# Probability rows scaled on GpSimd, score operands split once for two heads and placed by DMA, and forgetting attention's head factors made for two pairs at a time

## The chip, the cores and the metric

One Trainium2 chip; the kernel runs on one of its cores. The time is that of the whole program on the device, in microseconds (us). TensorE (PE), VectorE (DVE), ScalarE (ACT), GpSimd (POOL) and SyncE (SP) each run their own instructions in a fixed order; in this kernel SP issues nearly all transfers.

## The reference

Two transformer blocks over 512 positions of width 1024, in float32. The first has a feed-forward network, a mixing layer (three-branch sparse attention with 16 query heads of width 64, a gated convolution, attention to a memory of 256 rows) and a second feed-forward network. The second block has two layers: stick-breaking attention and forgetting attention, each followed by a feed-forward network and a gate. The parts that the change touches:

```python
def rms_norm(x, g):
    y = x * lax.rsqrt(jnp.mean(x * x, axis=-1, keepdims=True) + EPS)
    return y * g
# sparse attention, selected blocks and window, a head at a time
s = einsum('qd,kd->qk', q, k) * scale + bias;  p = masked_softmax(s);  o = p @ v
out = gate_c * o_c + gate_s * o_s + gate_w * o_w
# stick-breaking attention
z = q @ k.T * scale;  w = exp(log_sigmoid(z) + later(z));  o = w @ v
# forgetting attention: q and k normalized for each head
logits = q @ k.T * scale + fb[:, None] - f_cum[None, :];  o = softmax(causal(logits)) @ v
```

## The kernel before

Activations are stored transposed, 128 features by 512 positions to a tile. Float32 products are made from pairs: `split` writes a rounded part `h` (ACT) and the rest `lo` (DVE, `src - h`), and a dense product is three matmuls (`mm3`, L221 to L223). Weights come in chunks of 128x1024: a DMA into `raw` (L209), in forgetting attention a multiplication by the gain on POOL (L213), then the split into `wh` and `wl` (L191, L201), each of the three tiles with three buffers. One 128x512 result takes 24 matmuls.

For the scores of two heads that share a 128-row tile, `stacked` (rounded part and rest of one head above each other) and `doubled` (the rounded part twice, and the rest with zeros) make operands of all 128 rows; they split each half of 64 rows by itself, and in `doubled` POOL writes the zeros (L357) and copies the rounded half to the other half (L359). `scores` then takes two matmuls for a tile of 128 queries (L371, L372).

In sparse and forgetting attention a head goes this way: scores into PSUM bank `s`, a DVE pass that adds the bias and finds the extreme (L525), an exponential on ACT that sums the row (L527), the reciprocal of the sums (L922, L1147), the scaling of the four probability tiles (L925, L1149: 128x128, 128x256, 128x384, 128x512), ten transpositions on PE into bank `t` (L774), their splits into `pth` and `ptl`, and eight products with the values (L781, L782). The products of one head are kept back in `self.rest` and are written into the program after the next head's scores.

`head_stats` squares the tiles, sums them for each head on PE (L316) and calls `rstd`, which makes the inverse root with an exponential and one Newton step; `head_norm` spreads the factors over the rows on PE (L334, L335) and multiplies on DVE (L336). In forgetting attention `lead(t)` makes key and query tiles of pair `t` (and every second time values for two pairs) and their factors, `norm` normalizes them and makes the operands, and `forget_head` runs twice. `lead(t + 1)` is written between `norm` of pair `t` and its heads.

The program is written in this order, but a scheduler at build time sets the order on each engine by its own account of when things are ready, so dense products of later pairs stand between the steps of a head.

Of the kernel before, what the change touches and what calls it, by code (L numbers as in the profile page):

```python
# [17 lines left out]
S = 512  # L18
# [144 lines left out]
class Net:  # L163
# [90 lines left out]
    def rstd(self, out, ss, n, rows=P):  # L254

        nc = self.nc
        v = self.t(self.sb, S, "nrv")[:rows, :n]
# [80 lines left out]

    def stacked(self, pool, x, tag, scale=None, bufs=None):

        out = []
# [7 lines left out]
    def doubled(self, pool, x, tag, scale=None, bufs=None):  # L349

        nc = self.nc
        out = []
        for b in range(2):
            z = self.t(pool, S, f"{tag}d{b}", bufs, F32R)
            lo = self.t(pool, S, f"{tag}l{b}", bufs, F32R)
# [95 lines left out]
    def setup(self):  # L451
# [6 lines left out]
        nc.vector.memset(self.ones_d, 1.0 / D)  # L458
        self.h = [self.pair(sb, f"h{c}") for c in range(KC)]
# [227 lines left out]
    def compress_flat(self, pool, tn, xs):  # L687
# [4 lines left out]
        for k in range(4):  # L692
# [10 lines left out]
            fh, flo = self.pair(pool, "pt", S, 2)  # L703
# [82 lines left out]
    def nsa(self):  # L786
        nc, tc = self.nc, self.tc
        with self.pool("nsa", "right") as pool:
# [41 lines left out]
            for j in range(4):  # L830
                self.head_norm(ks[j], j, 1, st, self.col("kg"))
            for a in range(2):
                kn = [self.doubled(pool, ks[2 * br + a], f"k{br}") for br in range(2)]
# [63 lines left out]
    def nsa_heads(self, pool, a, r, qn, kn, V, pc, G):  # L897
        nc = self.nc
        for b in range(2):
# [12 lines left out]
            for br in range(2):  # L912
# [11 lines left out]
                for i in range(NT):  # L924
                    nc.vector.tensor_scalar(pr[i], pr[i], st[:, i : i + 1], None, op0=ALU.mult)  # L925
# [61 lines left out]
    def stick(self):  # L987
        nc, tc = self.nc, self.tc
        self.log_exp_tables()
        with self.pool("sbk", "left") as pool:  # L990
            self.tags = self.TAGS
            m, V, rT = [], {}, self.t(pool, NT, "rT")

            def lead(t):
# [11 lines left out]
                return self.doubled(pool, qk[0], "q", 0.125, 2), self.stacked(pool, qk[1], "k", None, 2)  # L1006
# [68 lines left out]
    def forget(self):  # L1075
# [3 lines left out]
        with self.pool("fox", "left") as pool:  # L1079
# [17 lines left out]
            def lead(t):  # L1097
                if t % 2 == 0:
                    V[t // 2] = self.values(pool, self.a["w_fv"][t // 2], rT, gs)
                xs = []  # L1100
                for w, g in (("w_fk", gs), ("w_fq", ga)):
# [102 lines left out]
```

## Time and profile before

| | |
|---|---|
| median of 3 runs | 2964.11 us (2963.78 to 2964.3) |
| the profiled execution, its own time | 2958.98 us |
| its span, first to last instruction | 2957.2 us |
| PE busy | 2890.5 us |
| DVE busy | 1741.1 us |
| ACT busy | 1247.7 us |
| POOL busy | 191.3 us |

The profiled execution lies 5.1 us (0.17%) under the median, and 1.8 us of it lie outside the span. The parts of the span that the change touches: sparse attention from about 560 to 1050 us, stick-breaking attention from about 1490 to 1760 us, forgetting attention from about 2220 to 2530 us. The rest is dense work. The end of a matmul in the trace is modelled, so that matmuls overlap in it; how fast they follow each other is read from their starts.

### The profile page before, as it was taken

The page shows a single profiled execution, that of the slowest core. Times are in us where ns is not written, and L with a number is a line of the kernel's source. Part 1 is how long each engine was busy: PE and PEld are TensorE (multiplying, and loading weights), DVE is VectorE, ACT ScalarE, POOL GpSimd, SP SyncE. Part 2 cuts the span into 40 slices and gives each one's busy share as a digit, 9 for nine tenths or more (in the row PEclk, how much of TensorE's full clock was granted, in tenths as well). Part 3 has the DMA queues.
Part 4 walks back from the last instruction along what each step waited for, and adds up shares of the span by engine and source line. Part 5 has one row for each costly group of instructions (what it writes and reads, how often), then busy time and mean ns, then how long its engine had stood idle before and what let it go on. Part 6 is the DMA issues. An engine that isn't in the chain of part 4 may idle for free.

```text
span 2957.2 us, 36647 instructions
## 1 busy us (share of the span) xinstructions
PE 2890.5 (98%) x13874; PEld 2360.8 (80%) x13874; DVE 1741.1 (59%) x2997; ACT 1247.7 (42%) x2130; POOL 191.3 (6%) x245
## 2 busy tenths in 40 slices
PE   8999999999999999999999999999998998999999
PEld 8888887787877888888888877888887776788887
DVE  7434345778868755343358886443458997543334
ACT  6322234345646544222246664232244665432223
POOL 0000000001011010000012100000004311000000
PEclk9999999999999999999999999999999999999999
DMA  7432342232232345323331135323332223523322
GB/s 228 119 100 93 102 133 90 91 123 75 82 98 65 90 157 171 100 94 96 110 108 44 51 107 178 98 95 95 92 122 92 72 64 115 181 97 100 93 87 98
DMA packets 115946, 310.84 MB, mean 105 GB/s; under 512 B 13959, under 2 KB 26759, under 8 KB 115768
## 3 DMA queue, kind: packets, MB, share of 16 engines
q1 hardware_dynamic: 115096, 307.17, 32.8%
q10 hardware_dynamic: 672, 1.32, 0.4%
q8 instruction: 109, 1.79, 0.2%
q14 instruction: 69, 0.57, 0.1%
HBM read 279.82 MB, written 28.61 MB: 104 GB/s over the span
## 4 chain that ended last, share of the span: by engine, by line
PE 88%; DVE 7%; ACT 2%; DMA 1%; issue 1%; POOL 0%; SPq 0%; DVEq 0%; POOLq 0%; ACTq 0%
PE d L223 10%; PE d L222 10%; PE d L221 10%; PE o L221 5%; PE o L223 5%; PE o L222 5%; PE s L221 5%; PE s L222 5%; PE t L223 5%; PE t L221 5%; PE t L222 5%; PE s L223 5%; PE t L774 2%; DVE wl L201 1%; PE s L371 1%
## 5 line engine op out<-in xcount | busy, mean ns | idle before, releaser
L191 ACT ACTIVATE wh<-raw 128x1024 fp32r<-128x1024 f32 (+3 forms) x499 | 493.7, 990 | 1248.4 <-PE d L222 343.8
L201 DVE TENSOR_TENSOR wl<-raw,wh 128x1024 fp32r<-128x1024 f32 (+3 forms) x499 | 573.5, 1150 | 308.8 <-ACT wh L191 306.0
L191 ACT ACTIVATE pth<-t 128x512 fp32r<-128x512 f32 x144 | 70.5, 524 | 58.3 <-PE t L774 57.7
L774 PE MATMUL t<-idn,pr 128*128 128x128 f32 x480 | 85.7, 286 | 8.4 <-DVE ptl L201 3.7
L201 DVE TENSOR_TENSOR ptl<-t,pth 128x512 fp32r<-128x512 f32 x144 | 81.9, 596 | 13.1 <-ACT pth L191 11.9
L213 POOL TENSOR_TENSOR raw<-raw,cols 128x1024 f32<-128x1024 f32 x25 | 52.8, 2116 | 543.6 <-DMA xd<-x 483.2
L774 PEld LDWEIGHTS t<-idn,pr 128*128 128x128 f32 x480 | 56.9, 142 | 30.6 <-DVE ptl L201 11.4
L781 PE MATMUL o<-ptl,V 128*128 128x512 f32 x192 | 63.0, 339 | 0.0
L525 DVE CUSTOM_DVE_ANT_0 pr<-s,tb 128x128 f32<-128x128 f32 (+3 forms) x128 | 59.8, 482 | 4.1 <-PE s L372 3.1
L782 PE MATMUL o<-pth,V 128*128 128x512 f32 x192 | 57.5, 326 | 0.0
L415 DVE TENSOR_TENSOR ta<-t,ta 128x512 f32<-128x512 f32 x22 | 15.2, 692 | 70.9 <-PE t L223 70.8
L415 DVE TENSOR_TENSOR ta<-s,ta 128x512 f32<-128x512 f32 x22 | 15.2, 691 | 70.2 <-PE s L223 70.2
L221 PE MATMUL d<-h0h,wh 128*128 128x512 f32 x138 | 55.9, 405 | 0.5 <-ACT qs L191 0.4
L414 ACT ACTIVATE ta<-ta 128x512 f32<-128x512 f32 x88 | 55.3, 629 | 2.3 <-DVE ta L413 2.1
L415 DVE TENSOR_TENSOR ta<-o,ta 128x512 f32<-128x512 f32 x22 | 15.2, 692 | 68.4 <-PE o L223 67.4
L415 DVE TENSOR_TENSOR ta<-d,ta 128x512 f32<-128x512 f32 x22 | 15.2, 691 | 68.1 <-PE d L223 67.4
L223 PE MATMUL d<-h0h,wl 128*128 128x512 f32 x138 | 54.4, 394 | 0.8 <-DVE wl L201 0.8
L222 PE MATMUL d<-h4l,wh 128*128 128x512 f32 x138 | 54.7, 397 | 0.0
L222 PE MATMUL d<-h0l,wh 128*128 128x512 f32 x138 | 54.7, 396 | 0.0
L223 PE MATMUL d<-h4h,wl 128*128 128x512 f32 x138 | 54.6, 396 | 0.0
L222 PE MATMUL d<-h7l,wh 128*128 128x512 f32 x138 | 54.4, 394 | 0.0
L222 PE MATMUL d<-h3l,wh 128*128 128x512 f32 x138 | 54.4, 394 | 0.0
(2175 smaller groups left out, 8921.3 us busy)
## 6 DMA issues: line engine op xcount, KB each, us to landing
raw<-in_f_in_dram SPq DMA_DIRECT2D x176, 512.0 KB
raw<-in_f_out_dram SPq DMA_DIRECT2D x64, 512.0 KB
raw<-in_f_out_dram SPq DMA_DIRECT2D x32, 384.0 KB
raw<-in_w_mg_dram SPq DMA_DIRECT2D x24, 512.0 KB
raw<-in_w_cv_dram SPq DMA_DIRECT2D x24, 512.0 KB
xd<-x SPq DMA_DIRECT2D x40, 256.0 KB
x<-xd SPq DMA_DIRECT2D x40, 256.0 KB
raw<-in_w_pg_dram SPq DMA_DIRECT2D x16, 512.0 KB
```

The lines of the kernel that those rows point to most:

```text
L191: nc.scalar.activation(h, src, AF.Copy, scale=1.0 if scale is None else scale)
L201: eng.tensor_tensor(lo, src, hb, op=ALU.subtract)
L213: nc.gpsimd.tensor_tensor(v, v, gain.unsqueeze(2).to_broadcast([P, gain.shape[1], n]), op=ALU.mult)
L221: mm(out, lh, rh, start=first, stop=False)
L222: mm(out, lh, rl, start=False, stop=False)
L223: mm(out, ll, rh, start=False, stop=last)
L414: nc.scalar.activation(ta, ta, AF.Silu)
L415: nc.vector.tensor_tensor(ta, pb, ta, op=ALU.mult)
L525: nc.vector.tensor_tensor_reduce(out=p, in0=src, in1=bias, op0=ALU.add, op1=ALU.min, scale=1.0, scalar=3e38, accum_out=m)
L774: nc.tensor.transpose(tp[:, d : d + P], pr[i][:, j * P : (j + 1) * P], self.ident)
L781: nc.tensor.matmul(po[:, j * P :], v(j), pl[:, c], start=first and j == 0, stop=False)
L782: nc.tensor.matmul(po[:, j * P :], v(j), ph[:, c], start=False, stop=last and j == NT - 1)
```

## The change

It does these things. (1) `rstd` adds EPS inside the logarithm's bias and inside the last multiplication, with one DVE instruction less. (2) `stacked` and `doubled` split all 128 rows at once into `hv` tiles, and DMAs of 64x512 (four for `stacked`, six for `doubled`) place the halves; the zeroed rows of the `lo` tiles are written once. These DMAs stand in SP's queue with the weight loads. (3) The four probability tiles of a head are scaled by POOL instead of DVE. (4) In forgetting attention `lead(u)` makes two pairs of keys and queries, with one `head_stats` for four tiles, and is called after every second `norm` only. (5) `pth`/`ptl` have one buffer instead of two.

```diff
     def rstd(self, out, ss, n, rows=P):
-        nc.vector.tensor_scalar(v, ss, EPS, None, op0=ALU.add)
-        nc.scalar.activation(r, v, AF.Ln)
+        nc.scalar.activation(r, ss, AF.Ln, bias=self.eps[:rows])
...
-        nc.vector.tensor_tensor(t, t, v, op=ALU.mult)
+        nc.vector.scalar_tensor_tensor(t, ss, EPS, t, op0=ALU.add, op1=ALU.mult)
...
+    def halves(self, pool, x, scale):
+        h, lo = self.pair(pool, "hv", bufs=2)
+        self.split(h, lo, x, scale)
+        return h, lo
     def stacked(self, pool, x, tag, scale=None, bufs=None):
...
-            self.split(z[own], z[other], x[own], scale)
+            nc.sync.dma_start(z[own].bitcast(F32), h[own].bitcast(F32))
+            nc.sync.dma_start(z[other].bitcast(F32), lo[own].bitcast(F32))
...
-            nc.gpsimd.memset(lo[other].bitcast(F32), 0.0)
-            self.split(z[own], lo[own], x[own], scale)
-            nc.gpsimd.tensor_scalar(z[other], z[own].bitcast(F32), 1.0, 1.0, op0=ALU.mult, op1=ALU.mult)
-            out.append((z, lo))
+            nc.sync.dma_start(z[own].bitcast(F32), h[own].bitcast(F32))
+            nc.sync.dma_start(z[other].bitcast(F32), h[own].bitcast(F32))
+            nc.sync.dma_start(los[b][own].bitcast(F32), lo[own].bitcast(F32))
+            out.append((z, los[b]))
...
-        ph, pl = self.pair(pool, "pt", 1280, 2)
+        ph, pl = self.pair(pool, "pt", 1280, 1)
...
-                    nc.vector.tensor_scalar(pr[i], pr[i], st[:, i : i + 1], None, op0=ALU.mult)
+                    nc.gpsimd.tensor_scalar(pr[i], pr[i], st[:, i : i + 1], 1.0, op0=ALU.mult, op1=ALU.mult)
...
+            def lead(u):
+                V[u] = self.values(pool, self.a["w_fv"][u], rT, gs)
                 xs = []
-                for w, g in (("w_fk", gs), ("w_fq", ga)):
...
+                for t in (2 * u, 2 * u + 1):
+                    for w, g in (("w_fk", gs), ("w_fq", ga)):
...
                 return xs, self.head_stats(xs, self.sel64, 1, pool=pool)
...
-                k, q = norm(*ahead)
-                if t + 1 < KC:
-                    ahead = lead(t + 1)
+                k, q = norm(t, *ahead)
+                if t % 2 and t + 1 < KC:
+                    ahead = lead(t // 2 + 1)
```

The order of PE near the end of forgetting attention, where the factors of pair 6 have been spread and its scores follow. `h`, `m` with a number are activations of a dense product, `kd`, `kl`, `qs` the score operands. Before, these rows stand ahead of the scores:

```order
L223 MATMUL d_21196<-h5h_81,wl_21201 128x512
L221 MATMUL d_21196<-h6h_83,wh_21200 128x512
L222 MATMUL d_21196<-h6l_84,wh_21200 128x512
L223 MATMUL d_21196<-h6h_83,wl_21201 128x512
L221 MATMUL d_21196<-h7h_85,wh_21200 128x512
L222 MATMUL d_21196<-h7l_86,wh_21200 128x512
L223 MATMUL d_21196<-h7h_85,wl_21201 128x512
L316 MATMUL s_21230<-nrq_21232,sr_156 16x512
L316 MATMUL s_21230<-nrv_21233,sr_156 16x512
L371 MATMUL s_21267<-kd_4118_21144,qs_4122_21156 128x256
```

They are the last of 48 dense matmuls of pair 7 that stand between the spreading (L334, L335) of pair 6 and its scores. Now the same place reads, from the last product of pair 5 on:

```order
L801 MATMUL o_21039<-pth_21040,V_19938 128x128
L221 MATMUL d_21651<-m4h_20574,wh_21654 128x512
L222 MATMUL d_21651<-m4l_20575,wh_21654 128x512
L223 MATMUL d_21651<-m4h_20574,wl_21655 128x512
L221 MATMUL d_21651<-m0h_21245,wh_21654 128x512
L222 MATMUL d_21651<-m0l_21246,wh_21654 128x512
L223 MATMUL d_21651<-m0h_21245,wl_21655 128x512
L388 MATMUL s_21281<-kd_4154_21259,qs_4158_21271 128x256
```

Six dense matmuls are left there, with the eight products of pair 5 ahead of them and the four spreading matmuls ahead of those; the dense work of pair 7 stands earlier, after the spreading of pair 5.

The order of DVE in a head of pair 0 of forgetting attention before (`st` are the reciprocals, `pr` the probability tiles, `nr`, `hr` the factors of the next pair):

```order
L1147 RECIPROCAL st_19058<-st_19058 128x4
L525 ISA pr_3650_19142,pr2m_19141<-s_19137,fb_19118 128x384
L525 ISA pr2m_19141 128x1
L264 TENSOR_TENSOR nrq_19042<-nrq_19042,nrv_19040 16x512
L1149 TENSOR_SCALAR pr_3624_19064<-pr_3624_19064,st_19058 128x128
L265 SCALAR_TENSOR_TENSOR nra_19039<-nrq_19042,nrr_19041 16x512
L1149 TENSOR_SCALAR pr_3627_19072<-pr_3627_19072,st_19058 128x256
L195 CAST hrh_19049<-nra_19039 16x512
L1149 TENSOR_SCALAR pr_3630_19080<-pr_3630_19080,st_19058 128x384
L201 TENSOR_TENSOR hrl_19050<-nra_19039,hrh_19049 16x512
L1149 TENSOR_SCALAR pr_3633_19088<-pr_3633_19088,st_19058 128x512
```

The four scalings stand among work for other heads. Now they stand in POOL's order, for the two heads of pair 0 with the gain multiplications of weights between them:

```order
L213 TENSOR_TENSOR raw_19946<-raw_19946,cols_67 128x1024
L1174 TENSOR_SCALAR pr_3649_19111<-pr_3649_19111,st_19105 128x128
L1174 TENSOR_SCALAR pr_3652_19119<-pr_3652_19119,st_19105 128x256
L1174 TENSOR_SCALAR pr_3655_19127<-pr_3655_19127,st_19105 128x384
L1174 TENSOR_SCALAR pr_3658_19135<-pr_3658_19135,st_19105 128x512
L213 TENSOR_TENSOR raw_20062<-raw_20062,cols_67 128x1024
L1174 TENSOR_SCALAR pr_3669_19173<-pr_3669_19173,st_19167 128x128
L1174 TENSOR_SCALAR pr_3672_19181<-pr_3672_19181,st_19167 128x256
```

A head's scaling has DVE's queue no longer ahead of it, but the weight multiplication that stands before it on POOL.

## Rows read from the trace of the kernel before

**Rows 1.** The page: busy time, share of the span and instructions of each engine.

```profile
PE 2890.5 (98%) x13874; PEld 2360.8 (80%) x13874; DVE 1741.1 (59%) x2997; ACT 1247.7 (42%) x2130; POOL 191.3 (6%) x245
```

**Rows 2.** Busy time by stretch: length; PE, PEld, DVE, ACT, POOL; clock.

```profile
700.00:1000.00 300.00, 289.55 (x1477) 230.97 (x1478) 247.19 (x623) 172.23 (x395) 35.42 (x32) 0.99 0.28 81
1500.00:1760.00 260.00, 258.92 (x1481) 218.56 (x1480) 202.91 (x416) 156.79 (x332) 39.45 (x96) 1.00 0.22 68
2220.00:2290.00 70.00, 60.32 (x347) 49.66 (x346) 57.06 (x88) 32.94 (x58) 28.40 (x25) 1.00 0.26 88
2290.00:2450.00 160.00, 153.35 (x876) 123.65 (x875) 148.71 (x301) 101.23 (x212) 41.87 (x40) 1.00 0.25 79
2450.00:2530.00 80.00, 68.17 (x308) 51.29 (x307) 61.56 (x125) 43.32 (x89) 8.57 (x6) 0.94 0.37 123
```

**Rows 3.** Waits of PE in 2210 to 2530: total us, times, longest.

```profile
PE s L371 <- DVE qs L203: 7.2, 4, 3.0
...
PE t L774 <- DVE pr L1149: 2.1, 4, 1.1
```

**Rows 4.** Waits of PE in 690 to 1000.

```profile
PE s L368 <- DVE cv L336: 3.0, 2, 2.7
PE t L774 <- DVE pr L925: 2.1, 3, 1.2
```

**Rows 5.** DVE groups, 2220 to 2530: count | busy us, mean ns | idle.

```profile
L1149 DVE TENSOR_SCALAR pr<-pr,st 128x128 f32<-128x128 f32 (+1 forms) x64 | 21.4, 375 | 0.1
L203 DVE SCALAR_TENSOR_TENSOR qs<-x,qs 64x512 fp32r<-64x512 f32 x16 | 17.5, 1097 | 0.5
L201 DVE TENSOR_TENSOR kl<-x,kd 64x512 fp32r<-64x512 f32 x16 | 16.1, 1009 | 0.3
...
L263 DVE SCALAR_TENSOR_TENSOR nrq<-nrr 16x512 f32<-16x512 f32 (+1 forms) x9 | 9.5, 1051 | 2.7 <-ACT nrr L262 2.7
...
L260 DVE TENSOR_SCALAR nrv<-s 16x512 f32<-16x512 f32 (+1 forms) x9 | 6.1, 677 | 0.9 <-PE s L316 0.8
```

**Rows 6.** Scaling on DVE in sparse attention.

```profile
L925 DVE TENSOR_SCALAR pr<-pr,st 128x128 f32<-128x128 f32 (+3 forms) x128 | 43.0, 396 | 0.2
```

**Rows 7.** Instructions of line 359: duration ns min/median/max.

```profile
L359 POOL TENSOR_SCALAR kd<-kd x16: 613/942/1138, 2271.2 to 2495.3; 64x512 fp32r<-64x512 f32 x16
```

**Rows 8.** Groups of POOL: count | busy us, mean ns | idle before.

```profile
L657 POOL TENSOR_TENSOR cv<-cv,rB 128x512 f32<-128x512 f32 x8 | 10.3, 1288 | 79.3 <-DVE cv L656 79.3
```

**Rows 9.** Timeline, forgetting attention: start, us, engine, [idle before <-releaser].

```profile
2308.61 5.26 POOL L213 TENSOR_TENSOR raw<-raw,cols 128x1024 f32<-128x1024 f32 x2 [5.49 <-DMA raw<-in_w_fv_dram]
...
2310.08 2.04 DVE L201 TENSOR_TENSOR nrr<-nra,nrq 128x512 fp32r<-128x512 f32 x1
```

**Rows 10.** Timeline of one head, its last score to its transpositions.

```profile
2500.25 0.69 DVE L525 CUSTOM_DVE_ANT_0 pr<-s,fb 128x512 f32<-128x512 f32 x1 [0.23 <-PE s L1144]
...
2502.24 1.27 DVE L1149 TENSOR_SCALAR pr<-pr,st 128x128 f32<-128x128 f32 x4
```

**Rows 11.** Timeline between the spreading of pair 7 and its scores.

```profile
2492.96 0.39 PE L335 MATMUL t<-hrl,selr 128*128 128x512 f32 x1
...
2496.97 0.36 PE L371 MATMUL s<-kd,qs 128*128 128x256 f32 x1 [3.04 <-DVE qs L203]
```

**Rows 12.** Timeline of dense matmuls with 512 columns.

```profile
2361.57 0.39 PE L221 MATMUL d<-h1h,wh 128*128 128x512 f32 x1
2361.79 0.39 PE L222 MATMUL d<-h1l,wh 128*128 128x512 f32 x1
```

**Rows 13.** Tile od: issue of a 64x512 transfer, ns min/median/max.

```profile
L932 SPq DMA_DIRECT2D od<-on x16: 451/452/501, 743.0 to 1049.3; - x16
```

**Rows 14.** Timeline of SP and DVE, a load and who waited for it.

```profile
1760.41 0.32 SPq L966 DMA_DIRECT2D qk<-xd  x1
...
1762.55 0.69 DVE L969 TENSOR_TENSOR qk<-d,qk 128x512 f32<-128x512 f32 x1 [1.39 <-DMA qk<-xd]
```

**Rows 15.** Busy time by stretch at the end of forgetting attention.

```profile
2480.00:2490.00 10.00, 7.05 (x28) 5.45 (x29) 8.05 (x23) 4.24 (x12) 0.00 (x0) 0.68 0.14 49
```

More of the change, by code (lines that the diff above doesn't have):

```diff
@@ L344, in stacked, with zeroed, doubled @@
             own, other = slice(64 * b, 64 * b + 64), slice(64 - 64 * b, 128 - 64 * b)
-            self.split(z[own], z[other], x[own], scale)
+            nc.sync.dma_start(z[own].bitcast(F32), h[own].bitcast(F32))
+            nc.sync.dma_start(z[other].bitcast(F32), lo[own].bitcast(F32))
             out.append(z)
         return out
-    def doubled(self, pool, x, tag, scale=None, bufs=None):
+    def zeroed(self, pool, tag, bufs=1):
+        out = []
+        for k in range(bufs):
+            zs = [self.t(pool, S, f"{tag}l{k}{b}", dt=F32R) for b in range(2)]
+            for b, z in enumerate(zs):
+                self.nc.gpsimd.memset(z[64 - 64 * b : 128 - 64 * b].bitcast(F32), 0.0)
+            out.append(zs)
+        return out
+    def doubled(self, pool, x, tag, los, scale=None, bufs=None):
         nc = self.nc
+        h, lo = self.halves(pool, x, scale)
         out = []
@@ L458, in setup @@
         nc.vector.memset(self.ones_d, 1.0 / D)
+        self.eps = self.t(sb, 1, "eps")
+        nc.vector.memset(self.eps, EPS)
         self.h = [self.pair(sb, f"h{c}") for c in range(KC)]
@@ L702, in compress_flat @@
                         fv[h, :, g, :31], xv, pe[h, 4 * k : 4 * k + 4].unsqueeze(2).to_broadcast([64, 4, 31]), op=ALU.add)
-            fh, flo = self.pair(pool, "pt", S, 2)
+            fh, flo = self.pair(pool, "pt", S, 1)
             self.split(fh, flo, fl)
@@ L831, in nsa @@
                 self.head_norm(ks[j], j, 1, st, self.col("kg"))
+            los = [self.zeroed(pool, f"k{br}")[0] for br in range(2)]
             for a in range(2):
-                kn = [self.doubled(pool, ks[2 * br + a], f"k{br}") for br in range(2)]
+                kn = [self.doubled(pool, ks[2 * br + a], f"k{br}", los[br]) for br in range(2)]
                 qs = []
@@ L1095, in forget, with norm @@
             self.transpose_rows(rT, self.rB)
-            def lead(t):
-                if t % 2 == 0:
-                    V[t // 2] = self.values(pool, self.a["w_fv"][t // 2], rT, gs)
+            los = self.zeroed(pool, "k", 2)
+            def lead(u):
+                V[u] = self.values(pool, self.a["w_fv"][u], rT, gs)
                 xs = []
-                for w, g in (("w_fk", gs), ("w_fq", ga)):
-                    ps = self.dbank()
-                    self.dense(ps, self.a[w][t], self.h, g)
-                    x = self.t(pool, S, "x", 4)
-                    nc.vector.tensor_tensor(x, ps, self.rB, op=ALU.mult)
-                    xs.append(x)
-                return xs, self.head_stats(xs, self.sel64, 1, pool=pool)
-            def norm(xs, st):
-                for z, gc in ((0, "fkg"), (1, "fqg")):
-                    self.head_norm(xs[z], z, 1, st, self.col(gc), tag="t")
-                return self.doubled(pool, xs[0], "k", None, 2), self.stacked(pool, xs[1], "q", -0.125, 2)
+                for t in (2 * u, 2 * u + 1):
+                    for w, g in (("w_fk", gs), ("w_fq", ga)):
+                        ps = self.dbank()
+                        self.dense(ps, self.a[w][t], self.h, g)
+                        x = self.t(pool, S, "x", 6)
+                        nc.vector.tensor_tensor(x, ps, self.rB, op=ALU.mult)
+                        xs.append(x)
+                return xs, self.head_stats(xs, self.sel64, 1, pool=pool)
+            def norm(t, xs, st):
+                z = 2 * (t % 2)
+                for j, gc in ((z, "fkg"), (z + 1, "fqg")):
+                    self.head_norm(xs[j], j, 1, st, self.col(gc), tag="t")
+                return self.doubled(pool, xs[z], "k", los[t % 2], None, 2), self.stacked(pool, xs[z + 1], "q", -0.125, 2)
             ahead = lead(0)
```

13 lines of the change are left out of this document (7 added, 6 removed).

## The prediction

> **What bounds the kernel now.** I read the engines' shares first. PE is busy for 98% of the span, no other engine for more than 59% [rows 1]. So the kernel is bounded by PE, and a change that takes no matmul away can only win or lose in the holes between matmuls. The stretches show where these are; a hole is the stretch's length less PE's busy time [rows 2]. In 300 us of sparse attention PE idles 10.4 us, in 260 us of stick-breaking 1.1 us, at the start of forgetting attention 9.7 us of 70, in its middle 6.65 us of 160, at its end 11.8 us of 80. DVE is busy for 149 us of the 160 in the middle, so there it is nearly a second bound: a wait for DVE in that stretch is one for its whole queue. The waits of PE name two places. In forgetting attention scores wait for the query operand (7.2 us in four waits), and transpositions for scaled rows (2.1 us in four) [rows 3]; in sparse attention 3.0 and 2.1 us [rows 4]. The rest of the holes is split over short waits. The change touches both places.
>
> **The change part by part.** The profiled execution took 2958.98 us, 0.17% under the median of 2964.11, and the sum is made against it. A difference under 0.2%, 5.9 us, can't be told from none.
>
> *Work that leaves DVE.* In forgetting attention 64 scalings of 375 ns go, 24.0 us. The 32 splits of half tiles, 16 by 1097 and 16 by 1009 ns, 33.6 us, become 16 over all rows. DVE's time goes by columns and not by rows: 16x512 takes 677 ns [rows 5] and 128x512 690 [rows 14]. So a split that isn't held up by POOL takes about 0.69 us, and 11 us remain. `head_stats` runs four times for eight, each time with one operation less. With six operations a call, of 677 to 1051 ns as the two of [rows 5], 4.4 us for each of eight calls become 3.7 for each of four: some 20 us go. Together DVE loses about 66 us in this layer. In sparse attention 128 scalings of 396 ns go, 50.7 us [rows 6].
>
> *The scaling on POOL.* Nothing in the trace has POOL scale 128 rows. Its nearest row is a one-input operation on 64x512, 613 ns at best and 942 in the median [rows 7]. A head has 1280 columns. By columns alone that is 1.53 us, by four instructions of the longest kind 2.45 us. The highest bound is the two-input operation on 128x512, 1288 ns [rows 8]: 3.2 us for 1280 columns. I take 1.7 us, near the best case, as it is the same kind of operation as [rows 7]. On DVE the four take 1.27 us [rows 10]. So the chain of a head from its last score to its transpositions, 3.26 us where nothing holds it up (2500.25 to 2503.51, [rows 10]), becomes 3.7 us, and up to 4.65 us where POOL or DVE holds it up.
>
> The Trainium skill speaks against this move: "GPSIMD Engine Reference", section "Performance versus the Vector engine", has DVE 1.96 times as fast in an elementwise addition of 2048 columns. By that the four scalings take 2.5 us instead of 1.27, an estimate, each chain is 0.8 us longer than I take it, and with 16 heads in forgetting attention half exposed my sum would be about 6 us higher, close to no change. The one-input rows of POOL say less, and no row here is of the shape itself.
>
> *What covers that chain.* While a head's rows are made PE does products of the head before and dense work. I counted the matmuls between a head's last score and its first transposition in the two orders and priced them by their spacing, 0.22 us for 512 columns [rows 12]. In sparse attention the cover falls from 5.8 to 4.9 us a head, still over 3.7. In forgetting attention it falls from 5.4 to 3.3 us, since dense work of the next pairs now stands in one lump after every second `norm`. There the chain is longer than its cover in most heads: between 0.4 and 1.3 us short, half of it seen by PE on some ten heads, +4.5 us in the middle. DVE's relief works against it: of the 6.65 us of holes there nearly all are waits for its queue, and I take 6 us back. Middle: **-1.5 us**, between -6.6 (every hole closed) and +9 (ten heads 1.6 us short and nothing back).
>
> *The start.* `lead(0)` now makes four tiles, so between the first `norm` and its scores the order has some 60 dense matmuls, 24 before. Of the 9.7 us of holes the waits for operands there go: **-4 us**, between -5.5 and 0.
>
> *The operands by DMA.* For a pair ten transfers stand in SP's queue; the first head needs eight of them (six for `kd` and `kl`, two for its `qs`). Issue takes 451 ns each [rows 13], 3.6 us, and from the last issue to its use 2.1 us go by [rows 14]. From the spreading on that is 6 to 6.6 us, with the first split ahead and a part of the landings under the next issues. Behind these ten stand weight loads in SP's queue; they come 4.5 us later, but `raw` has three buffers, and I price that at nothing; without that lead PE would lose the 4.5 us once a pair. Where the dense lump stands after `norm` (pairs 1, 3 and 5) it hides all of this. For pairs 2 and 4 about 48 matmuls of 256 columns stand there, 5.7 us, just enough.
>
> *The end.* Pairs 6 and 7 have no lead left. Pair 6 had 48 dense matmuls of 512 columns, 10.9 us, between spreading and scores; now it has six of them and eight products, about 2.6 us: +3.4 us. Pair 7 has no cover in either kernel, and before its scores came 4.0 us after the spreading [rows 11]; now 6.5: +2.5 us. The transpositions of these four heads wait longer by +1.5 us in all. End: **+7 us**, between +1 (the stretch's own holes of 11.8 us take the moved work) and +16: PE's granted clock was 0.68, between the two levels of 1.2 and 2.4 GHz, in a stretch in which it was busy for 7.05 us of 10 [rows 15], so longer waits may cost matmul time too.
>
> *Sparse attention* has cover left and DVE 50.7 us freer, so its two kinds of wait go, and some of the short ones: **-6 us**, between -15 (the 10.4 us of the 300 shown, and the like share outside) and +10 (a chain 0.3 us short in all 32 head-branches). *Stick-breaking* has 1.1 us of holes in all: **-1 us**, to +3 if operands come late. *`rstd`* is one DVE operation of 677 ns shorter a call [rows 5], exposed in about three of its calls: **-2 us**, between -3 and 0. *The single buffer of `pt`* makes a head's splits wait for the eight products before; half of the +4.5 us above stands for it.
>
> Sum: -4 - 1.5 + 7 - 6 - 1 - 2 = -7.5 us, so 2951.5 for the profiled execution, and on the median **2957 us**.
>
> **The rivals.**
>
> A, the sum above, -3 to -14 us: 40%. About a quarter of it lies within 5.9 us of before.
>
> B, DVE's relief closes nearly all holes: start -5.5, middle -6.6, end +1, sparse -8, the rest -3: -22 us, 2942. For it speaks DVE's 93% in the middle [rows 2]; against it that the chain of one head is made of several engines' steps, which a free queue doesn't shorten. 17%.
>
> C, the change doesn't do what it is meant for: PE has no fewer matmuls, holes closed in one place open in the next, 2958 to 2970: 18%. For it speaks that the end loses about what the start and the sparse layer win.
>
> D, slower: POOL takes 3.2 us for four scalings, as its two-input row [rows 8]. Then transpositions wait in nearly every head of forgetting attention: middle +9, end +11, sparse 0, the rest -7: +13 us, 2977. It decides from about 2 us for the four on. For it speaks also that the multiplications of weights by their gain, 2.6 us each, stand in POOL's queue between heads [rows 9]. 15%.
>
> E, slower by hold-ups of DVE. A DVE operation with two inputs takes 2.04 us beside POOL's multiplication [rows 9], where one of its size takes 0.69 us [rows 14]. 48 chains of scaling in the two layers could each hold one such operation up by 1.35 us, 65 us of DVE time, about half of what it was freed of. If one in four stands on a path to PE, 16 us are lost; the relief of the start, the middle and the sparse layer is gone, and the end's +7 and the other -3 stay: +20 us, 2984. Against it: most of the DVE operations around a head's chain read PSUM or run outside of it. 10%.
>
> The rule behind E is in the Trainium skill, "SBUF — State Buffer", section "Who interferes with whom": a DVE instruction with two inputs in SBUF and a GpSimd one that reads SBUF exclude each other, and the later one waits for the other's end. The trace agrees with 2.04 beside 0.69 us. By that rule POOL's scalings wait as well for DVE's splits.
>
> **How the numbers follow.** The time is A's. Outside of 2938 to 2978 lie E, a part of D and the far end of B, about 2 in 10. Faster by over 0.2%: 30% from A and 17% from B, 47%. Within: 10% from A and 18% from C, 28%. Slower: D and E, 25%. A's own range is 2950 to 2961.
>
> **What would show it.** In the profile after: POOL's four scalings near 1.7 us (over 2.5, and D holds); DVE 60 us or more under 149 + 57 + 62 us in the three stretches of forgetting attention; the waits for `qs` gone at the start, and grown to 3 us and more before pairs 6 and 7, now released by DMAs; transpositions waiting for POOL in the middle by 0.5 us each; sparse attention with under 7 us of holes in its 300. I am wrong if the lumps of dense work make the middle lose more than the sparse layer wins, or if the scheduler's order, which I count cover in, isn't kept up by the transfers.

## The result: 1.35% slower, and the profile after

The changed kernel takes 3005.89 us (median of 4 runs, 3000.64 to 3007.05), the one before 2964.2 in the same comparison: a ratio of 1.0135, 95% interval 1.0117 to 1.0153. The forecast was 2957 us, in a range of 2938 to 2978.

The page of the changed kernel: its span, then busy time, share and instructions of each engine [rows 1].

```profile
span 3005.2 us, 37131 instructions
...
PE 2915.0 (97%) x13873; PEld 2373.1 (79%) x13874; DVE 1620.6 (54%) x2718; ACT 1218.1 (41%) x2078; POOL 241.1 (8%) x361
```

DVE is freed of 120 us, as wanted, and POOL has 50 us more. PE does as many matmuls in 24.5 us more of busy time, and has holes of 90 us where it had 67. Part of the busy time is the clock: the mean granted clock fell from 0.996 to 0.990, and span times what is missing to 1, an estimate of what the clock costs, is 12 us before and 30 after. These two profiles show the difference near its largest: over all runs the clock is 0.992 to 0.997 before and 0.990 to 0.994 after.

The traces have 13,874 matmuls before and 13,873 after, so the start of the n-th one tells where the 48 us of span came in. At the 3,000th the changed kernel is 4.4 us ahead (627.3 for 631.8), at the 5,500th, past sparse attention, 18.5 behind (1170.2 for 1151.6), at the 8,500th, past stick-breaking, 15.8, at the 10,500th, at the start of forgetting attention, 17.7, and at the 12,250th, behind it, 47.6. So sparse attention lost 23 us and forgetting attention 30; stick-breaking won 3. Some 6 of the 48 us belong to the profile of the kernel before, which is that much shorter than its median in the later comparisons (2964.6 to 2966.1 us). A later run, b_pt1, has the same order of PE and the same median, and its profile is 0.2 us behind that of before in sparse attention, but 6.4 behind between the 10,500th matmul and the 11,000th.

Busy time by stretch: length; PE, PEld, DVE, ACT, POOL; granted clock [rows 2]. The last three are the start, the middle and the end of forgetting attention.

```profile
700.00:1000.00 300.00, 281.58 (x1390) 220.54 (x1390) 193.10 (x470) 155.17 (x358) 85.11 (x121) 0.98 0.35 96
2236.00:2310.00 74.00, 66.45 (x369) 55.84 (x368) 55.55 (x60) 29.77 (x44) 27.65 (x19) 0.98 0.35 101
2310.00:2470.00 160.00, 144.13 (x783) 114.92 (x782) 101.13 (x207) 84.39 (x181) 48.16 (x56) 0.97 0.38 108
2470.00:2580.00 110.00, 91.20 (x398) 65.31 (x397) 66.53 (x141) 53.10 (x115) 13.37 (x24) 0.88 0.47 143
```

In sparse attention the holes grew from 10.4 to 18.4 us of 300, and in the middle of forgetting attention from 6.65 to 15.9 of 160, although DVE is busy there for 101 us where it was for 149. A freer queue did not close holes. At the end the clock went as well (0.88; 0.50 to 0.87 in the four stretches of 10 us from 2510 on):

```profile
2510.00:2520.00 10.00, 3.96 (x13) 2.44 (x13) 4.82 (x11) 2.63 (x7) 0.00 (x0) 0.68 0.81 220
2520.00:2530.00 10.00, 8.65 (x34) 5.66 (x34) 5.12 (x17) 5.94 (x17) 3.20 (x7) 0.64 0.40 140
2530.00:2540.00 10.00, 6.05 (x28) 3.85 (x26) 6.57 (x10) 4.55 (x8) 0.92 (x2) 0.87 0.30 68
2540.00:2550.00 10.00, 7.46 (x26) 5.35 (x27) 3.34 (x15) 4.20 (x14) 1.39 (x4) 0.50 0.46 117
```

Waits of PE in sparse attention, 690 to 1060 (total us, times, longest) [rows 4]:

```profile
PE t L793 <- POOL pr L945: 11.4, 20, 1.3
```

and in forgetting attention, 2236 to 2580 [rows 3]:

```profile
PE d L221 <- DVE V L203: 5.5, 2, 2.7
PE t L793 <- DVE ptl L201: 5.0, 7, 1.0
PE s L388 <- DMA qs<-hvl: 5.0, 2, 2.7
PE s L314 <- DVE nrv L201: 4.7, 3, 1.8
PE t L793 <- POOL pr L1174: 4.4, 12, 1.0
```

The transpositions' waits for scaled rows went from 2.1 us in three to 11.4 us in twenty in sparse attention. A wait in this view begins only where PE's modelled busy time ends, so I also took the time from each matmul's start to the next, less what is usual in the kernel before (227 ns behind 512 columns, 120 behind 256, 109 behind a transposition). By that 35 of the 48 us stand right before the ten transpositions of a head, 22.5 in sparse and 12.7 in forgetting attention.

Groups of POOL (count | busy us, mean ns | idle before): the four scalings of a head.

```profile
L945 POOL TENSOR_SCALAR pr<-pr,st 128x512 f32<-128x512 f32 x32 | 22.3, 698 | 0.0
L945 POOL TENSOR_SCALAR pr<-pr,st 128x384 f32<-128x384 f32 x32 | 20.4, 637 | 0.0
...
L945 POOL TENSOR_SCALAR pr<-pr,st 128x256 f32<-128x256 f32 x32 | 15.5, 483 | 0.1
...
L945 POOL TENSOR_SCALAR pr<-pr,st 128x128 f32<-128x128 f32 x32 | 12.4, 388 | 67.2 <-DVE st L943 19.9 <-PE s L389 17.6 <-ACT pth L191 16.8
```

The four take 2.15 us in the median of the heads, in both layers. A head near the end of sparse attention, in order of time, shows what its rows pass through:

```profile
1011.96 0.68 DVE L544 CUSTOM_DVE_ANT_0 pr<-s,tb 128x512 f32<-128x512 f32 x1
...
1013.53 0.18 DVE L942 RECIPROCAL st<-st 128x4 f32<-128x4 f32 x1
1013.63 1.19 DVE L201 TENSOR_TENSOR wl<-raw,wh 128x1024 fp32r<-128x1024 f32 x1
1013.67 2.28 POOL L667 TENSOR_TENSOR cv<-cv,rB 128x512 f32<-128x512 f32 x1 [5.40 <-DVE cv L666]
1014.74 1.23 DVE L943 TENSOR_TENSOR st<-st,G 128x4 f32<-128x4 f32 x1
1016.17 0.37 POOL L945 TENSOR_SCALAR pr<-pr,st 128x128 f32<-128x128 f32 x1 [0.22 <-DVE st L943]
```

Between the reciprocal and the first scaling stand the split of a weight and the multiplication of four columns, which takes 1.23 us beside POOL's operation and 0.16 in the median of all 32. The first transposition, 4.6 us after the pass over the last scores began, then waits 1.31 us for POOL, and the next ones between the tiles.

### The profile page after: what moved, and what is told of

The parts are those of the page before. It is cut to its first block, busy times and chain, and to the rows that moved or that the text cites. A ratio compares the mean times of both kernels' runs of the same rounds, so it can differ in the third digit from the quotient of the medians.

```text
span 3005.2 us, 37131 instructions
## 1 busy us (share of the span) xinstructions
PE 2915.0 (97%) x13873; PEld 2373.1 (79%) x13874; DVE 1620.6 (54%) x2718; ACT 1218.1 (41%) x2078; POOL 241.1 (8%) x361
## 4 chain that ended last, share of the span: by engine, by line
PE 58%; DVE 3%; issue 2%; DMA 2%; POOL 1%; ACT 1%; SPq 0%; POOLq 0%; DVEq 0%; ACTq 0%
PE d L221 6%; PE d L222 6%; PE d L223 6%; PE t L222 4%; PE t L223 4%; PE o L221 4%; PE t L221 4%; PE o L223 4%; PE o L222 4%; PE s L221 4%; PE s L223 4%; PE s L222 4%; PE t L793 1%; PE s L388 1%; POOL pr L1174 1%
## 5 line engine op out<-in xcount | busy, mean ns | idle before, releaser
L793 PE MATMUL t<-idn,pr 128*128 128x128 f32 x480 | 98.0, 297 | 26.3 <-POOL pr L945 11.4
L945 POOL TENSOR_SCALAR pr<-pr,st 128x128 f32<-128x128 f32 (+3 forms) x128 | 68.0, 551 | 67.3 <-DVE st L943 19.9
L221 PE MATMUL d<-h4h,wh 128*128 128x512 f32 x136 | 54.5, 401 | 0.0
L223 PE MATMUL d<-h1h,wl 128*128 128x512 f32 x136 | 54.2, 398 | 0.0
L221 PE MATMUL d<-h6h,wh 128*128 128x512 f32 x136 | 54.1, 398 | 0.0
L222 PE MATMUL d<-h5l,wh 128*128 128x512 f32 x136 | 54.0, 397 | 0.0
L221 PE MATMUL d<-h5h,wh 128*128 128x512 f32 x136 | 53.9, 397 | 0.0
L223 PE MATMUL d<-h5h,wl 128*128 128x512 f32 x136 | 53.9, 397 | 0.0
```

Source lines behind the costliest of these rows:

```text
L221: mm(out, lh, rh, start=first, stop=False)
L222: mm(out, lh, rl, start=False, stop=False)
L223: mm(out, ll, rh, start=False, stop=last)
L793: nc.tensor.transpose(tp[:, d : d + P], pr[i][:, j * P : (j + 1) * P], self.ident)
L945: nc.gpsimd.tensor_scalar(pr[i], pr[i], st[:, i : i + 1], 1.0, op0=ALU.mult, op1=ALU.mult)
```

## The experiments

Each kernel was compared with the kernel before; times are medians, ratios have 95% intervals. Names in b_ are edits of the kernel before, in a_ of the changed one.

**The parts.** The theory that these traces suggested: the scaling on POOL costs most (S), with the operands by DMA beside the pairs (O) and the single buffer (P) as rivals.

a_dve, scaling back on DVE:

```diff
-  nc.gpsimd.tensor_scalar(pr[i], pr[i], st[:, i : i + 1], 1.0, op0=ALU.mult, op1=ALU.mult)
+  nc.vector.tensor_scalar(pr[i], pr[i], st[:, i : i + 1], None, op0=ALU.mult)
```

> The changed kernel with the four scalings of a head back on DVE. Theory S (the scaling on POOL costs most: four take 2.06 us there and 1.27 on DVE, and PE's holes inside the ten transpositions grew from 3.6 to 16.1 us in sparse and from 6.6 to 14.9 us in forgetting attention): about 25 us come back, 2975 to 2985, and sparse attention is within 5 us of its time before. Rival O (operands by DMA and lumps of dense work in forgetting attention): under 8 us come back, 2998 or more. Rival P (the single buffer of the transposed rows): under 8 us as well, and sparse attention stays some 20 us longer.

Measured: 2970.86 us, 1.0016 (1.0007 to 1.0026); 35 us come back, 10 more than S expected, and sparse attention is now some 6 us shorter than before (between the 3,000th and the 5,500th matmul).

b_pool, the reverse edit in the kernel before:

> The kernel before with the scaling of the four tiles of a head on POOL in sparse and forgetting attention, and nothing else. Theory S: slower by 20 to 30 us, 2985 to 2994, with transpositions waiting for POOL. Rival O and rival P: within 6 us of 2964, as DVE gets free by what POOL takes longer.

Measured: 3007.99 us, 1.0144 (1.0129 to 1.016): this part alone costs as much as the whole change. Its waits of PE, in sparse attention and in forgetting attention:

```profile
PE t L774 <- POOL pr L925: 10.0, 18, 1.7
```

```profile
PE t L774 <- POOL pr L1149: 10.8, 24, 1.3
```

b_ops_pt1, parts (2) and (5) of the change:

```diff
-            self.split(z[own], z[other], x[own], scale)
+            nc.sync.dma_start(z[own].bitcast(F32), h[own].bitcast(F32))
+            nc.sync.dma_start(z[other].bitcast(F32), lo[own].bitcast(F32))
```

> The kernel before with the operands split once for two heads and placed by DMA, and with one buffer for the transposed rows (the operand tiles leave no room for two). Theory S: within 6 us of 2964. Rival O: slower by 10 us or more, in forgetting attention. Rival P: slower by some 20 us, in sparse attention.

Measured: 2950.15 us, 0.9951 (0.9936 to 0.9966). The operands by DMA gain, which no theory had said; this is the fastest version measured. Waits of PE in forgetting attention, 2220 to 2570: the 7.2 us for `qs` [rows 3] are one wait of 2.8.

```profile
PE t L793 <- DVE ptl L201: 3.7, 5, 1.1
PE s L390 <- DMA qs<-hvl: 2.8, 1, 2.8
```

b_lead, part (4) of the change, with the operands as before:

```diff
-                return self.doubled(pool, xs[0], "k", None, 2), self.stacked(pool, xs[1], "q", -0.125, 2)
+                return self.doubled(pool, xs[z], "k", None, 2), self.stacked(pool, xs[z + 1], "q", -0.125, 2)
...
-                if t + 1 < KC:
-                    ahead = lead(t + 1)
+                if t % 2 and t + 1 < KC:
+                    ahead = lead(t // 2 + 1)
```

> The kernel before with keys and queries of two pairs made at once in forgetting attention, and one head_stats for the four tiles. Theory S: slower by 5 to 12 us, all of it at the end, where the two last pairs have no dense work left. Rival O: slower by 15 us or more, over the middle and the end. Rival P: within 6 us of 2964.

Measured: 2976.61 us, 1.0035 (1.0023 to 1.0048), as S expected in size, but not where: by the starts of matmuls 18 us come in the middle and 2 at the end. By the spacing of starts 14 us stand before scores and 7 before transpositions. The same view:

```profile
PE s L371 <- DVE qs L203: 13.9, 5, 4.0
PE t L774 <- DVE ptl L201: 7.8, 7, 1.2
```

b_pt1, part (5) of the change alone:

```diff
-        ph, pl = self.pair(pool, "pt", 1280, 2)
+        ph, pl = self.pair(pool, "pt", 1280, 1)
```

> The kernel before with one buffer for the transposed rows in place of two. If the operands by DMA alone gained b_ops_pt1's 15 us: 2964 to 2970, as the splits of a head now wait for the products before. If the single buffer gained a part by shifting the order: below 2962.

Measured: 2963.49 us, 0.9994 (0.9985 to 1.0003). No change, so rival P falls and the 15 us are the operands'.

b_rstd, the shorter `rstd` alone, part (1) of the change:

```diff
-        nc.vector.tensor_scalar(v, ss, EPS, None, op0=ALU.add)
-        nc.scalar.activation(r, v, AF.Ln)
+        nc.scalar.activation(r, ss, AF.Ln, bias=self.eps[:rows])
...
-        nc.vector.tensor_tensor(t, t, v, op=ALU.mult)
+        nc.vector.scalar_tensor_tensor(t, ss, EPS, t, op0=ALU.add, op1=ALU.mult)
```

> The kernel before with the shorter rstd alone. By the trace of the changed kernel the stretch before 600 us was 4 us shorter: 2958 to 2962. If that came from the operands instead, which b_ops_pt1 has too with 3.6 us less there: 2962 to 2966. If its other order of instructions costs what a_best1 is longer than b_ops_pt1: 2968.

Measured: 2974.94 us, 1.0032 (1.0022 to 1.0042). One instruction less costs 10 us. In its trace the transposition of `rB` at the start of forgetting attention waits 5.0 us (1.5 before), and more waits for scores came up. Why is open: the operation that adds EPS while it multiplies takes 676 ns on 16x512, no more than others of its size, and the logarithm that reads PSUM 679 for 628.

**Why the scaling costs.** Theory L: the rows come too late from POOL. Rival K: POOL holds up DVE. Rival M: the order, in which dense work leaves the time of a head's chain.

b_poolq, a quarter of each tile's columns scaled on POOL, the rest left unscaled:

```diff
-  nc.vector.tensor_scalar(pr[i], pr[i], st[:, i : i + 1], None, op0=ALU.mult)
+  nc.gpsimd.tensor_scalar(pr[i][:, : 32 * (i + 1)], pr[i][:, : 32 * (i + 1)], st[:, i : i + 1], 1.0, op0=ALU.mult, op1=ALU.mult)
```

> The kernel before with the scaling on POOL, but of a quarter of each tile's columns only (the rest stays unscaled); four instructions of POOL stay on the path, with some 1.1 us in place of 2.06 to 2.2. Counted in the two orders, the cover of a head falls as with the whole scaling on POOL, to 4.6 us in sparse and 3.5 us in forgetting attention. Theory L with POOL's duration as the cause: within 10 us of 2964. Rival M (the order: transpositions are placed earlier as soon as the scaling leaves DVE, whatever POOL takes): 2980 or more. Rival K: 2975 to 2990.

Measured: 3005.39 us, 1.0137 (1.0122 to 1.0152). The four scalings of a head now take 1.4 us on POOL in sparse attention and 1.6 in forgetting attention, where DVE took 1.6 and 1.5, and the cost is the same. So POOL's duration isn't it. Its groups of POOL in sparse attention:

```profile
L925 POOL TENSOR_SCALAR pr<-pr,st 128x64 f32<-128x64 f32 x32 | 12.3, 385 | 0.1
L925 POOL TENSOR_SCALAR pr<-pr,st 128x128 f32<-128x128 f32 x32 | 11.9, 371 | 0.0
L925 POOL TENSOR_SCALAR pr<-pr,st 128x96 f32<-128x96 f32 x32 | 11.0, 344 | 0.0
L925 POOL TENSOR_SCALAR pr<-pr,st 128x32 f32<-128x32 f32 x32 | 10.8, 338 | 104.0 <-DVE st L923 80.5 <-ACT pr L527 6.7 <-DVE kc L854 6.5
```

b_dummy, POOL multiplies a tile that nobody reads, beside the scaling on DVE:

```diff
   nc.vector.tensor_scalar(pr[i], pr[i], st[:, i : i + 1], None, op0=ALU.mult)
+  nc.gpsimd.tensor_scalar(dm[:, : (i + 1) * P], self.rB[:, : (i + 1) * P], st[:, i : i + 1], 1.0, op0=ALU.mult, op1=ALU.mult)
```

> The kernel before, and beside the four scalings on DVE POOL makes four more of the same size on a tile that nobody reads; the order of PE is the same as before. Theory L (a head's rows come too late from POOL for the transpositions that stand next in PE's order): within 8 us of 2964, since nobody waits for POOL. Rival K (POOL holds up DVE's operations with two inputs in SBUF, and these hold up PE): 2984 or more, half or more of the 42 us that moving the scaling cost.

Measured: 2981.4 us, 1.0059 (1.0044 to 1.0074), between L and K. PE, DVE, ACT and SP have the order of before here, so these 17 us come from POOL's work beside theirs. Most of it is hold-up of DVE's scalings, which have one input: in both layers together they took 74.7 us and now 91.7, and no other group grew by more than 2.4. In the trace 15 us stand before the transpositions, which wait for these scalings. Its groups of DVE, where before had 478 and 475 ns:

```profile
L926 DVE TENSOR_SCALAR pr<-pr,st 128x512 f32<-128x512 f32 x32 | 22.8, 712 | 0.0
...
L1152 DVE TENSOR_SCALAR pr<-pr,st 128x512 f32<-128x512 f32 x16 | 10.3, 645 | 0.0
```

So this experiment made a hold-up that the change doesn't have, as its scalings are off DVE. It shows that POOL does hold up DVE, and at a cost to PE. What is held up in the changed kernel itself can be read from its trace: of DVE's groups in sparse attention that both kernels have, only the multiplication of four columns grew by more than 0.4 us, from 184 to 295 ns in the mean, 3.6 us in all; it stands on the way of every head.

```profile
L943 DVE TENSOR_TENSOR st<-st,G 128x4 f32<-128x4 f32 x32 | 9.4, 295 | 0.4
```

b_hyb, the 128x512 tile on POOL, three on DVE:

```diff
-  for i in range(NT):
-      nc.vector.tensor_scalar(pr[i], ...)
+  for i in (3, 0, 1, 2):
+      if i == 3:
+          nc.gpsimd.tensor_scalar(pr[i], ...)
+      else:
+          nc.vector.tensor_scalar(pr[i], ...)
```

> The kernel before with the scaling of the 128x512 tile on POOL and of the other three on DVE, beside each other: 0.7 us on POOL, 0.85 on DVE. Theory L: faster or the same, 2950 to 2966, as the rows are ready earlier than with all four on DVE. Rival M: 2975 or more, since the cover falls from 5.4 to 4.5 us in forgetting attention. Rival K: 2970 to 2980.

Measured: 2987.55 us, 1.0078 (1.0063 to 1.0093): in M's range, and against L. It doesn't decide between M and K, though. The three scalings that stayed on DVE took 64.7 us where they had taken 51.8, held up by POOL's, and a head's rows come 0.3 to 0.4 us earlier, about what the cover falls by (the table further down). Its groups of DVE, where before had 346 and 299 ns:

```profile
L928 DVE TENSOR_SCALAR pr<-pr,st 128x256 f32<-128x256 f32 x32 | 15.8, 493 | 0.0
L928 DVE TENSOR_SCALAR pr<-pr,st 128x128 f32<-128x128 f32 x32 | 15.6, 487 | 0.2
```

b_poolord and b_dveord hold the matmuls in a given order, by edges that only set the order on PE (`ORDER` is a table of the 13,861 matmuls of the program):

```diff
         Net(ctx, tc, aps, out).run()
+        mm = sorted((i for i in nc.cur_bb.bb.instructions if isinstance(i, mybir.InstMatmult)), key=lambda i: int(i.name[2:]))
+        at = [mm[k] for k in np.frombuffer(zlib.decompress(base64.b85decode(ORDER)), "<u2")]
+        info = mybir.DependencyInfo(mybir.DependencyClass.NoSync, mybir.DependencyReason.DATA)
+        for one, two in zip(at, at[1:]):
+            tc.add_manual_dep(two, one.name, info, reason="order")
```

In the traces PE's order is then that of the other kernel, matmul for matmul. The other engines' orders move with it: DVE's in b_poolord differs from b_pool's in 370 of 2805 places. First b_poolord:

> The kernel before with the scaling on POOL as in b_pool, and with all matmuls held in PE's order of before by edges of order only. The cover of a head is again 5.76 us in sparse and 5.42 us in forgetting attention. Theory M (the move takes dense work out from under a head's chain, and that is what PE waits for): most of b_pool's 42 us is gone; what is left is the hold-up that b_dummy showed and POOL's longer chain, 2975 to 2988. Theory L (POOL's rows come too late whatever the order): 3000 or more. If M and the freer DVE both count: below 2970.

Measured: 2982.17 us, 1.0055 (1.0038 to 1.0072): 26 of b_pool's 42 us come back with the same work on POOL. Before transpositions b_pool had lost 38 us, and 15 of them are left. Then b_dveord:

> The kernel before with the scaling on DVE, and with all matmuls held in the order that PE has in b_pool, with a cover of 5.05 and 3.92 us a head. Theory M: slower by what the order costs, 2980 to 2995. Theory L: within 8 us of 2964, since no scaling is on POOL.

Measured: 3008.33 us, 1.0146 (1.0131 to 1.0161): the whole loss, and no scaling on POOL: 28 us stand before transpositions, 12 before scores. Its transpositions now wait for DVE as they did for POOL (690 to 1065; this kernel's lines stand two further down):

```profile
PE t L776 <- DVE pr L927: 9.7, 18, 1.6
PE s L373 <- DVE pr3m L527: 4.3, 5, 1.6
```

a_poolord, the changed kernel in a_dve's order:

> The changed kernel, scaling on POOL, with all matmuls held in the order that PE has when the scaling is on DVE (a_dve, 2971). Theory M: most of the 35 us between a_dve and the changed kernel goes and the hold-up of some 17 us stays: 2982 to 2992. If all parts together leave the rows too late in any order: 3000 or more. If the hold-up is hidden by DVE's freer queue: 2966 to 2975.

Measured: 2984.46 us, 1.0063 (1.0045 to 1.0081): 21 of the 35 us between a_dve and the changed kernel.

**Where the theory of the cover ends.** Three kernels in the order of before, which has the most cover. b_rstdord:

> b_rstd with all matmuls held in PE's order of before. The cover in forgetting attention is 5.42 us a head again and not 4.52. Theory M (the order is what costs): 2956 to 2963, one DVE operation less in some calls gained. Rival R (the operation that adds EPS while it multiplies is itself the slower way, or the logarithm that reads PSUM is): 2970 or more.

Measured: 2988.24 us, 1.0078 (1.0063 to 1.0093): 13 us longer than b_rstd in its own order. b_ops_ord:

> b_ops_pt1 (2950) with all matmuls held in PE's order of before, whose cover is 5.76 and 5.42 us a head where its own order has 5.48 and 4.43. Theory M: 5 to 15 us faster than b_ops_pt1, 2935 to 2945. If its own order fits its own chains better: 2950 or more.

Measured: 2987.38 us, 1.0075 (1.006 to 1.009): 37 longer than b_ops_pt1. best_ord:

> a_best1 (2955: operands by DMA, single buffer, shorter rstd, scaling on DVE, a pair at a time) with all matmuls held in PE's order of before. Theory M: the shorter rstd now gains instead of costing, so it is the fastest, 2930 to 2943. If rstd costs in itself: some 5 us longer than b_ops_ord.

Measured: 3014.69 us, 1.0164 (1.0148 to 1.0181), for a_best1's 2954.61. Theory M missed all three; the first two lie in the ranges of the other theories named, though the slower operation of R is not in b_rstd's trace. By the spacing of starts none of the three loses more than 1 us before transpositions, and they lose 19, 24 and 43 us before scores. The waits of PE in b_rstdord, forgetting attention, show more:

```profile
PE t L776 <- DVE ptl L203: 7.4, 10, 1.1
PE s L371 <- DVE qs L205: 7.1, 4, 3.0
PE s L371 <- DVE pr3m L527: 5.3, 5, 1.6
PE s L371 <- DVE pr1m L527: 4.3, 3, 1.7
```

No transposition waits long for its row; a head's first tile is scaled 3.1 us before PE comes to it, in the mean. Scores wait for `pr3m` and `pr1m` in their place: the passes of DVE that empty the bank `s`. DVE's order was, it seems, made for a quicker chain and does the scalings first. So in these runs an order of PE was only good with the orders of the other engines made with it. It follows that b_dveord's 44 us can't all be put on the lost cover: its 12 us before scores are of this kind. The gains of b_poolord and a_poolord came in spite of such a disturbance.

**What the parts are worth together.** a_best1 leaves parts (3) and (4) out of the change:

> The changed kernel with the scaling back on DVE and keys and queries made a pair at a time as before; the operands by DMA, the single buffer and the shorter rstd stay. If the parts add up, 15 us from the operands and 2 to 4 from rstd: 2944 to 2950, the fastest so far. If rstd gives nothing beside the operands: 2950. If the operands by DMA gained only by the free place in DVE's queue that rstd needs too: 2955.

Measured: 2954.61 us, 0.9969 (0.9958 to 0.998), 4 us longer than b_ops_pt1, where the intervals still touch: the shorter `rstd` adds nothing to the operands' gain and may take some of it back, as it costs alone.

a_lead1 undoes part (4) in the changed kernel:

```diff
-                if t % 2 and t + 1 < KC:
-                    ahead = lead(t // 2 + 1)
+                if t + 1 < KC:
+                    ahead = lead(t + 1)
```

> The changed kernel with keys and queries made a pair at a time as before. If the parts count as they do alone: b_lead's 11 us come back, 2992 to 2998. If the pairs and the operands by DMA cost more together: 2980 to 2990. If the freer DVE hides it: 3000 or more.

Measured: 2995.99 us, 1.01 (1.0085 to 1.0115): the pairs cost 10 us here too, as they do alone.

a_oldop undoes part (2):

```diff
-            nc.sync.dma_start(z[own].bitcast(F32), h[own].bitcast(F32))
-            nc.sync.dma_start(z[other].bitcast(F32), lo[own].bitcast(F32))
+            self.split(z[own], z[other], x[own], scale)
```

> The changed kernel with the operands split by halves and copied by POOL as before, and no DMAs for them. If the parts count as they do alone: 15 us longer, 3017 to 3025. If the operands by DMA cost as much at the end, beside the pairs, as they gain before: 3000 to 3010. If POOL's copies of halves, now in one queue with the scalings, come late as well: 3030 or more.

Measured: 3003.89 us, 1.0123 (1.0106 to 1.014), 2 us from the changed kernel: beside the other parts the operands by DMA gain nothing. By the starts of matmuls the changed kernel is 2 to 3 us shorter than this one in each of sparse attention, stick-breaking and the middle of forgetting attention, and 7 us longer at the end (11.7 for 4.3 over before).

## Why the prediction was wrong

What the sum left out is best seen in one table. "Cover" is the matmul time between a head's last score and its first transposition, counted in the trace's order of PE with the usual spacings named above; this gives 0.4 to 0.5 us less in forgetting attention than the prediction's count. "Ready" is the mean time in the trace from the start of the pass over the 512-column scores to the end of the last scaling. Both are in us a head, sparse / forgetting. "Short" is ready less cover, summed over 32 and 16 heads; "before transpositions" is the time lost there against the kernel before, by the spacing of starts; the last column is the measured change of the medians.

| kernel | cover | ready | short | before transpositions | change |
|---|---|---|---|---|---|
| before | 5.78 / 4.93 | 5.57 / 5.60 | 4 | 0 | 0 |
| b_ops_pt1 | 5.63 / 4.00 | 5.27 / 5.05 | 5 | 0 | -15 |
| a_best1 | 5.53 / 3.56 | 5.14 / 4.50 | 3 | -3 | -10 |
| a_dve | 5.53 / 3.26 | 5.14 / 4.85 | 13 | 5 | +5 |
| b_rstd | 5.78 / 4.01 | 5.56 / 4.96 | 8 | -1 | +10 |
| b_lead | 5.78 / 3.48 | 5.57 / 4.90 | 16 | 7 | +11 |
| b_dummy | 5.78 / 4.93 | 5.97 / 5.92 | 22 | 15 | +17 |
| b_hyb | 5.59 / 4.26 | 5.23 / 5.21 | 4 | 12 | +23 |
| a_lead1 | 4.77 / 2.67 | 5.57 / 4.80 | 59 | 35 | +30 |
| b_poolq | 4.76 / 3.64 | 5.03 / 5.32 | 35 | 29 | +41 |
| changed kernel | 4.77 / 2.90 | 5.57 / 4.97 | 58 | 35 | +42 |
| b_pool | 4.95 / 3.60 | 5.36 / 6.38 | 57 | 38 | +42 |

The kernels with all scaling on POOL stand apart in the last three columns. For the rest the cover explains little: b_ops_pt1 and b_rstd gain and lose elsewhere, b_lead loses most before its scores, and b_hyb's 12 us are not in its means.

**The step that failed** is "In sparse attention the cover falls from 5.8 to 4.9 us a head, still over 3.7". The 3.7 came from a head at the very end, with no other work in DVE's and ACT's queues [rows 10]. Over all heads of the sparse layer the rows were ready 5.57 us after the pass began already before, and still are. Cover and chain had been level, and 1.0 us of cover lost in 32 heads comes to 32 us; 22.5 us were lost before the transpositions of this layer, and the layer lost 23 where I had -6. The chain is in large part a head's place in two queues in order, and the same plan that sets PE's order sets these places. The bound of 4.65 us for a held-up chain was too low by the prediction's own prices as well: with 3.2 us on POOL 3.26 becomes 5.2. In the same way ten heads 1.6 us short, half of it seen, are 8 us and not the 9 of the middle's range.

**The middle**, -1.5 us, lost 18 by the starts. By their spacing 13 us stand before transpositions, and 5.5 are two waits for splits of the values `V` (0.5 before), for which the sum had no term.

**Relief of DVE**, -6 us in the middle: it came (223 us of DVE in the three stretches for 267, 44 less and not 66) and bought no time. The rows got ready earlier in forgetting attention (4.97 for 5.60) but the cover shrank by more (2.90 for 4.93).

**POOL's chain**: 2.15 us where I took 1.7, a size wrong inside my bounds. Rival D had the sign and forgetting attention as a place, but nothing for sparse attention, and its mechanism, POOL's duration deciding from 2 us on, falls with b_poolq, which has DVE's duration and the full cost. What counts is that the move takes the scaling out of DVE's queue in the plan: dense matmuls are then placed elsewhere, and the real chain doesn't shorten with it. b_poolord shows this most directly, with 26 of 42 us back by PE's old order. Why the scheduler places them so was not looked into.

**Rival E**, hold-ups: the trace shows them, in all 3.6 us of DVE time on the way of sparse attention's heads, so they are a small part of the 23 us there. In forgetting attention splits for the sums of squares grew by 8 us (`nrv` 690 to 1486 ns, `nrr` 858 to 1100); what PE lost by them isn't settled. The held order leaves 18 of the 42 us (b_poolord), in which POOL's longer chain is too, and the disturbance of a foreign order.

**The start**, -4 us: the waits for `qs` went from it as forecast. From the 10,500th matmul to the 11,000th nothing was won against the profile of before, and 6 us against that of b_pt1, so one profile can't tell whether the forecast came; two waits of 1.6 and 1.5 us stand there for the sums of four tiles (`nrv`, `nrr`).

**The end**, +7 us: the mechanism held (two waits for `qs`, released by DMAs, 5.0 us, beside 2.3 and 2.9 for the last splits `m0h` and `m1h`), and with the clock at 0.50 to 0.87 it came to some 12 us from the 11,750th to the 12,250th matmul, within my bounds. a_dve has 12 there.

**The pairs** cost 10 to 11 us with and without the other parts, in the middle, where I had half of 4.5; alone they cost more by scores that wait for `qs` (13.9 us for 7.2) than by transpositions. **`rstd`**, -2: alone +10. **Stick-breaking**, -1: -3. **The buffer of `pt`**: nothing, as b_pt1 shows, where I had put half of 4.5 us on it. **The operands by DMA** gain 15 us alone, in sparse attention too, where I had forecast them as a cost only: most likely since one split of 128 rows halves DVE's and ACT's work in front of the scores; no run took that apart. The changed kernel loses this again, as a_oldop shows: 7 us of it at the end, before dense matmuls that wait for the last splits and weights (7 us by the spacing of starts, none in a_oldop). Why these come late is open.

The forecast's own test (less than 7 us of holes in sparse attention's 300) showed it wrong at once: 18.4.

## What to carry to other kernels

Measure the chain that is to be covered over all its occurrences, with the queues in it, and compare it with the cover that the new order leaves; a chain timed where the engines are empty makes any cover look enough. Where a scheduler sets the order, moving work to an idle engine changes the order on all of them, and that can cost more than the work itself (41 us in b_poolq, for scalings of the same duration as on DVE); try each part alone, since parts that look like relief (a shorter `rstd`, fewer sums) cost and one that looked like overhead (ten transfers for a pair) gained. A good order of one engine could not be carried to another version here without those of the rest (b_rstdord, b_ops_ord, best_ord).

## What the runs showed of the hardware

POOL's scaling has a high floor: 338 ns for 32 columns of 128 rows (b_poolq), 698 for 512 (changed kernel). And a DVE scaling with a single input of float32 in SBUF is held up by POOL as well: 712 ns for 128x512 beside POOL's, 478 alone (b_dummy). I had counted on that for two inputs only. The Trainium skill, "SBUF — State Buffer", section "Who interferes with whom", lists tensor_scalar among the operations that can take the port pair that DVE shares with GpSimd; these numbers agree.
